# The order of the mixer's last three tiles in a pooling-mixer and gated-FFN trunk

## The chip, the cores and the metric

One core of a Trainium2 chip runs the whole program. The metric is device microseconds (us) of that core, as the median of several runs. TensorE is called PE in the profile, its weight loads PEld, VectorE DVE, ScalarE ACT, GpSimd POOL, and SyncE, which issues most DMAs, SP.

## The reference

The input is 1024 tokens of 1024 features in float32, and there is one layer of depth. It computes:

```
h  = rms_norm(x, norm_mix_g)
y  = pool_scale * (windowed mean of h (2, 4, 8, 16 tokens) - h) @ pool_w + pool_b     (4 groups of 256 features)
x1 = x + y
n  = rms_norm(x1, norm_ffn_g)
h2 = causal depthwise conv of width 3 over (n @ w_in)      w_in: 1024 x 5632
out = x1 + (silu(gate) * val) @ w_out                      val, gate: the halves of h2; w_out: 2816 x 1024
```

## The kernel before

**Stages.** Eight token tiles of 128 rows pass through the mixer. Then comes the first FFN product, 44 column blocks of 128 handled as 22 pairs n, and last the second product. Both are seven-product (Winograd) schemes: each 2 x 2 block product is made of seven products P1 to P7 of sums of blocks. Each of those takes its operands split in a head (rounded to float32r by ScalarE) and a remainder (source minus head, VectorE), and is 12 matmuls of 128 x 512.

**The mixer, tile j** (line numbers are those of the profile). `mixer_window` (L221) makes the window sums on TensorE (psd). `mixer_out` (L240) multiplies by the pool weights (psy, L247 and L250), adds the residual on VectorE (x, L253), stores it, and asks ScalarE for the row's square sum (junk, L154) and square root (L155), VectorE for the small steps after them (st, L156 to L159). `ffn_norm` (L257) writes the normalised tile (n2, L261). `ffn_operand` (L272) turns it with eight transposes into a PSUM pair of banks (pst, L276).

**What is made of a turned tile.** Tiles 0 to 3 give the FFN's blocks B11 and B21 with their splits. Tiles 4 to 7 give, together with tile j - 4, the block sums in n2f: `b22` is copied out by ScalarE (L287), then VectorE subtracts `b12` (in pst) from `b11` (L288), ScalarE and VectorE split that sum into T1 (L289: head L295, remainder L296), and VectorE makes two more differences (L290, L291). The first of those two is the last reader of the tile's PSUM banks.

**The FFN's weight side.** `prep_in` (L332) splits a weight block or a sum of weight blocks (S1 to S4) into a head and a remainder (`split`, L74, lines L76 and L77). For the first two pairs the sums themselves are made by accumulating DMAs; from the third pair on VectorE adds them (L310).

**The products around the change.** `events` (L418) is an order written by hand: P1 of pairs 0 and 1 (into banks X0, X1), P2 of both (X0, X1 again), P5 of both (T1 with S1, into Z0, Z1), P3 of both (B22 with S4), then P6, P7, P4 of pair 0 and of pair 1, and pairs 2 to 21 after them. The first three events stand in the mixer's loop, for its steps 8, 10 and 11. P5's banks Z lie in the PSUM space that the mixer's pool (ps_p, with pst) gives back, so their first matmul needs the last readers of pst to be done. A weight head takes a slot of a ring of seven (`hl`); x7 occupies one such slot until n2_7 has been made.

**What sets the order.** A scheduler orders the instructions of each engine; the code gives it the dependencies, and `tc.issue_after(mark)` queues what is recorded inside it behind the marked instruction on that instruction's engine (order only, no wait). Each engine then works through its own queue in that order, so an instruction that waits holds up all behind it.

Of the kernel before, what the change touches and what calls it, by code (L numbers as in the profile page):

```python
# [18 lines left out]
NS = S // P  # L19
NK = D // P  # L20
# [28 lines left out]
def trunk_kernel(ctx: ExitStack, tc: tile.TileContext, x, consts, par, rows, pool_w, w_in, w_out, out):  # L49
    nc = tc.nc  # L50
# [14 lines left out]
    def bank2(name):  # L65
        return ps_p.tile([P, 2 * NH], F32, tag="ps", name=name)
# [77 lines left out]
    ident = cst[:, :FAC]  # L144
# [4 lines left out]
    marks = {}  # L149
# [69 lines left out]
    ds, gains = {}, []  # L219
# [37 lines left out]
    def ffn_norm(j):  # L257
        x1, r = n2s[j]
        n2 = n2s[j] = pp.tile([P, D], F32, tag="n2", name=f"n2_{j}", bufs=2)
        nc.vector.tensor_tensor(r[1], r[0], r[1], ALU.mult)  # L260
        nc.vector.scalar_tensor_tensor(n2, x1, r[1], gains[0], op0=ALU.mult, op1=ALU.mult)  # L261
# [7 lines left out]
    for b in ("B11", "T1", "B21"):  # L269
        nops[b] = nop_tile(nop_a, b)  # L270

    def ffn_operand(j):  # L272
        n2 = n2s.pop(j)
        ps = bank2(f"pst{j}")
        for c in range(NK):
            nc.tensor.transpose(ps[:, c * P : (c + 1) * P], n2[:, c * P : (c + 1) * P], ident)  # L276
        cols = slice(j * P, (j + 1) * P)
        ps3 = ps.rearrange("p (c s) -> p c s", c=NK)
        lo, hi = slice(0, 4), slice(4, 8)
        if j < NS // 2:  # L280
# [6 lines left out]
        nc.scalar.activation(b22, ps3[:, hi, :], AF.Copy)  # L287
        sub(b11, b11, b12)  # L288
        split_n(nops["T1"], b11, cols0)  # L289
        sub(n2f[:, lo, cols], b22, b12)  # L290
        sub(b21, b22, b21)  # L291

    def split_n(t, src, cols=slice(None), ks=slice(None)):
        h = t[:, 0, ks, cols]
        nc.scalar.activation(h, src, AF.Copy)  # L295
        nc.vector.tensor_tensor(t[:, 1, ks, cols], src, h.bitcast(F32), ALU.subtract)  # L296


    order = [j + k * NP2 for j in range(NP2) for k in range(2)]
    raws, sums, aops = {}, {}, {}  # L300
# [3 lines left out]
        nc.sync.dma_start(raws[n], w_in[order[n]])  # L304

    def sub(out, a, b):
        nc.vector.tensor_tensor(out, a, b, ALU.subtract)  # L307

    def add(out, a, b):
        nc.vector.tensor_tensor(out, a, b, ALU.add)  # L310
# [1 line left out]
    def tmp(name):  # L312
        return work.tile([P, NH], F32, tag="sum", name=name, bufs=3)
# [18 lines left out]
    def prep_in(n, op):  # L332
        a11, a12, a21, a22 = (raws[n][:, i, k * NH : (k + 1) * NH] for i in range(2) for k in range(2))
        if op in ("S1", "S2") and (n, "S3") not in sums:
            s3 = sums[n, "S3"] = tmp(f"S3_{n}")
            add(s3, a11, a21)
            add(a21, a21, a22)
        if op in ("S2", "S4") and (n, "S2") not in sums:
            sums[n, "S2"] = a11
            add(a11, a21, a11)  # L340
        if op == "S4" and (n, "S4") not in sums:
            add(a12, a12, a11)
        if op == "S3":
            src = sums[n, "S3"]
        else:
            src = {"A11": a11, "A12": a12, "S1": a21, "A22": a22, "S2": a11, "S4": a12}[op]
        aops[n, op] = split(src, f"{op}s_{n}")
        if op == "A22" and n + 2 < NF:
            load_in(n + 2)

    def product(bank, a, b, opens):
        m = 0
        for k in range(4):
            ks = slice(k * P, (k + 1) * P)
            for i, l in ((0, 0), (0, 1), (1, 0)):
                nc.tensor.matmul(bank, a[:, i, ks], b[:, l, k, :], start=opens and m == 0, stop=m == 11, skip_group_check=not opens)  # L356
# [8 lines left out]
    def small(tag, name, bufs):  # L365
        return work.tile([P, NH], F32, tag=tag, name=name, bufs=bufs)

    def step(n, p):
        a, b, z = STEPS[p]
        opens = p in ("P1", "P6", "P5")  # L370
        if opens:
            pool = ps_x if z == "X" else ps_yz
            banks[n, z] = pool.tile([P, NH], F32, tag=z, name=f"{z}{n}")
        bank = banks[n, z]
        product(bank, aops.pop((n, a)), nops[b], opens)
        tt = nc.vector.tensor_tensor
        if p == "P1":
            hid[n, "q1"] = small("q1", f"q1_{n}", 2)
            nc.scalar.activation(hid[n, "q1"], bank, AF.Copy, scale=-1.0)
        elif p == "P2":  # L380
            hid[n, "a"] = work.tile([P, S], F32, tag="ha", name=f"ha{n}", bufs=1)
            nc.scalar.activation(hid[n, "a"][:, :NH], bank, AF.Copy)
        elif p == "P6":
            hid[n, "q2"] = tmp(f"q2_{n}") if n < 2 else late.tile([P, NH], F32, tag="q2", name=f"q2_{n}", bufs=2)
            tt(hid[n, "q2"], bank, hid[n, "q1"], ALU.subtract)
            if n < 2:
                tt(hid[n, "a"][:, NH:], banks[n, "Z"], hid[n, "q2"], ALU.add)
        elif p == "P5":
            hid[n, "r"] = left.tile([P, NH], F32, tag="r", name=f"r_{n}", bufs=2)
            tt(hid[n, "r"], hid[n, "q1"], bank, ALU.subtract)  # L390
        elif p == "P7":
            hid[n, "b"] = late.tile([P, S], F32, tag="hb", name=f"hb{n}", bufs=1)
            tt(hid[n, "b"][:, NH:], hid[n, "r"], bank, ALU.subtract)
# [67 lines left out]
    for j in range(2, NS + 4):  # L461
        if 2 < j < NS:
            mixer_norm(j)
        if 1 <= j - 1 < NS and j > 2:
            mixer_window(j - 1)
        if 1 <= j - 2 < NS:
            mixer_out(j - 2)
        if 0 <= j - 2 < NS:
            ffn_norm(j - 2)
        if 0 <= j - 4 < NS:  # L470
            ffn_operand(j - 4)
        if j in (4, 6):
            load_in(j // 2 - 2)
            sums_in(j // 2 - 2, 0)
        if 5 <= j <= 8:
            with tc.issue_after(marks[j - 2]), tc.issue_after(marks[f"b{j - 3}"]):
                prep_event(j - 5)
        if j in (7, 8):
            sums_in(j - 7, 1)
        if j in (8, 10, 11):  # L480
            event((8, 10, 11).index(j))
        with tc.issue_after(marks["edges"]):
            stat(j + 1)
            stat(j + 2)
# [15 lines left out]
    for ks in halves:  # L500
# [24 lines left out]
    def take(name):  # L525
# [113 lines left out]
    for k in range(-SLOOK, len(oevents)):  # L639
        p, f = oevents[k + SLOOK] if k + SLOOK < len(oevents) else (None, 0)  # L640
# [8 lines left out]
        with tc.issue_after(lasts[-1]) if lasts else nullcontext():  # L649
# [12 lines left out]
            p, f = oevents[k]  # L662
# [8 lines left out]
        set_, opens = chains[p]  # L671
# [17 lines left out]
        for i, g, c, bank in steps:  # L689
            a, b = oops[p, g]  # L690
            alone = opens and (p, i) != ("P4", 3)
            for m, (u, v) in enumerate(((0, 0), (0, 1), (1, 0))):
# [3 lines left out]
                    start=opens and first, stop=g == NP2 - 1 and m == 2, skip_group_check=not alone,  # L696
# [80 lines left out]
```

## Time and profile before

| | |
|---|---|
| Median of 3 runs | 705.21 us (705.0 to 705.26) |
| The profiled execution: its time, its span | 705.07 us, 702.9 us |
| PE, DVE, ACT busy in the span | 99%, 85%, 49% |
| PE's waits of the last mixer tiles and the first products | 1.2 us and 0.2 us, both at the start of P5 (Z) |
| Granted TensorE clock | 1.00 in all stretches asked |

In the rows of the timeline the first number is the start in us from the start of the span, the second the duration, then engine, line, operation, output and inputs by name without numbers (n is n2, a T or S stands for all tiles of that letter), partitions x elements and the count. In brackets is the idle time of the engine ahead of it and who ended it. Rows of VectorE operations of the same kind overlap a little: the next begins before the one ahead has ended.

### The profile page before, as it was taken

The numbers are of one execution on the slowest core, as the hardware profiler recorded it, in microseconds if no ns is written. First come the engines' busy times: TensorE is split into PE (matmuls) and PEld (weight loads), VectorE is DVE, ScalarE is ACT, GpSimd is POOL, SyncE is SP. The second block draws the span as 40 slices with busy tenths as digits, with TensorE's granted clock in tenths as the row PEclk, the third lists the DMA queues.
The fourth block names the chain that finished last, engine by engine and source line by source line (L and its number), as shares of the span: only waits on it lengthen the run. The fifth ranks groups of instructions, "written<-read, shape, count | busy, mean of one in ns | idle before, by whom it ended". The sixth has DMA issues, their size and how long they took to land.

```text
span 702.9 us, 8496 instructions
## 1 busy us (share of the span) xinstructions
PE 694.4 (99%) x3159; PEld 573.6 (82%) x3159; DVE 599.8 (85%) x884; ACT 343.1 (49%) x515; POOL 13.6 (2%) x32
## 2 busy tenths in 40 slices
PE   8999999999999999999999999999999999999997
PEld 5898788888888888888888888888888888888886
DVE  4688999999888888888888888876887988999985
ACT  5596546545444544444544444454554444444441
POOL 3110000000000000000000000000000000000000
PEclk9999999999999999999999999999999999999999
DMA  9953122132121122222222222229989700122121
GB/s 306 321 149 99 48 95 90 66 143 81 71 88 58 69 87 90 91 90 91 90 90 90 78 72 89 90 83 342 329 309 334 270 29 0 61 91 89 61 105 61
DMA packets 32586, 86.01 MB, mean 122 GB/s; under 512 B 3592, under 2 KB 5152, under 8 KB 29728
## 3 DMA queue, kind: packets, MB, share of 16 engines
q1 hardware_dynamic: 31296, 83.34, 33.2%
q0 software_dynamic: 1248, 2.11, 1.8%
q8 instruction: 25, 0.41, 0.2%
q14 instruction: 17, 0.14, 0.1%
HBM read 63.41 MB, written 19.92 MB: 119 GB/s over the span
## 4 chain that ended last, share of the span: by engine, by line
PE 95%; DMA 2%; DVE 1%; ACT 1%; issue 0%; SPq 0%; POOL 0%; DVEq 0%
PE oP L694 30%; PE Y L356 26%; PE Z L356 17%; PE X L356 16%; PE psy L247 3%; PE psd L176 2%; DMA x_edge<-in_x_dram 1%; PE pst L276 1%; DMA bias_hl<-rows_raw 1%; PE psy L250 1%; DVE n2f L307 0%; PE ps_edges L176 0%; DVE T L296 0%; PE ps_gain L214 0%; DVE n L261 0%
## 5 line engine op out<-in xcount | busy, mean ns | idle before, releaser
L694 PE MATMUL oP<-oBP,oAP 128*128 128x512 f32 (+1 forms) x924 | 208.9, 388 | 0.0
L694 PEld LDWEIGHTS oP<-oBP,oAP 128*128 128x128 f32 x924 | 172.9, 188 | 36.1 <-DVE oBP L77 0.3
L356 PE MATMUL Z<-T,S1s 128*128 128x512 f32 x264 | 64.1, 390 | 1.4 <-ACT T L295 1.2
L356 PE MATMUL X<-B,A11s 128*128 128x512 f32 x264 | 64.3, 390 | 0.0
L356 PE MATMUL Y<-T,S2s 128*128 128x512 f32 x264 | 64.0, 390 | 0.0
L356 PE MATMUL X<-B,A12s 128*128 128x512 f32 x264 | 63.5, 389 | 0.0
L356 PE MATMUL Y<-T,S3s 128*128 128x512 f32 x264 | 63.4, 389 | 0.0
L356 PE MATMUL Y<-T,A22s 128*128 128x512 f32 x264 | 63.4, 389 | 0.0
L356 PE MATMUL Z<-B,S4s 128*128 128x512 f32 x264 | 63.2, 389 | 0.0
L356 PEld LDWEIGHTS Z<-T,S1s 128*128 128x128 f32 x264 | 49.3, 188 | 12.6 <-ACT T L295 1.6
L356 PEld LDWEIGHTS Y<-T,S2s 128*128 128x128 f32 x264 | 49.4, 188 | 10.8 <-ACT S2s L76 0.4
L356 PEld LDWEIGHTS Y<-T,S3s 128*128 128x128 f32 x264 | 49.5, 188 | 10.3
L356 PEld LDWEIGHTS Y<-T,A22s 128*128 128x128 f32 x264 | 49.6, 188 | 10.3
L356 PEld LDWEIGHTS Z<-B,S4s 128*128 128x128 f32 x264 | 49.5, 188 | 10.3
L356 PEld LDWEIGHTS X<-B,A12s 128*128 128x128 f32 x264 | 49.5, 188 | 10.2
L356 PEld LDWEIGHTS X<-B,A11s 128*128 128x128 f32 x264 | 49.4, 188 | 10.2
L76 ACT ACTIVATE oBP<-blk 128x512 fp32r<-128x512 f32 x53 | 33.5, 633 | 49.1 <-PE oP L694 32.2
L77 DVE TENSOR_TENSOR oBP<-blk,oBP 128x512 fp32r<-128x512 f32 x53 | 36.7, 692 | 13.0 <-ACT oBP L76 13.0
L414 ACT ACTIVATE gate<-gate 128x1024 f32<-128x1024 f32 x22 | 23.3, 1061 | 44.8 <-DVE gate L405 44.5
L76 ACT ACTIVATE oAP<-blk 128x512 fp32r<-128x512 f32 x55 | 34.1, 621 | 18.9 <-DVE blk L307 15.9
L310 DVE TENSOR_TENSOR win<-win 128x512 f32<-128x512 f32 x60 | 41.3, 689 | 1.1
L77 DVE TENSOR_TENSOR oAP<-blk,oAP 128x512 fp32r<-128x512 f32 x55 | 37.8, 687 | 2.6 <-ACT oAP L76 2.6
(125 smaller groups left out, 942.5 us busy)
## 6 DMA issues: line engine op xcount, KB each, us to landing
win<-in_w_in_dram SPq DMA_DIRECT2D x22, 1024.0 KB, 4.8
g_dram<-val SPq DMA_DIRECT2D x22, 512.0 KB, 2.6
blk<-g_dram SPq DMA_DIRECT2D x33, 256.0 KB, 5.3
blk<-in_w_out_dram SPq DMA_DIRECT2D x31, 256.0 KB, 5.8
A12s<-g_dram SPq DMA_DIRECT2D x22, 256.0 KB, 5.2
B21s<-in_w_out_dram SPq DMA_DIRECT2D x22, 256.0 KB, 2.7
x<-in_x_dram SPq DMA_DIRECT2D x8, 512.0 KB, 9.5
x_dram<-x SPq DMA_DIRECT2D x8, 512.0 KB, 2.6
```

What stands on the lines that cost most here:

```text
L76: nc.scalar.activation(t[:, 0, :], src, AF.Copy)
L77: m = nc.vector.tensor_tensor(t[:, 1, :], src, t[:, 0, :].bitcast(F32), ALU.subtract)
L176: m = nc.tensor.matmul(ps[:, c * P : (c + 1) * P], src[:, c * P : (c + 1) * P], weights[:, c // 2, :], start=True, stop=True)
L247: nc.tensor.matmul(o, dh[:, c, :], wps[:, c, :], start=c % 4 == 0, stop=False, skip_group_check=True)
L250: m = nc.tensor.matmul(ps[:, cols], ones, bias_hl[:, cols], start=False, stop=True, skip_group_check=True)
L276: nc.tensor.transpose(ps[:, c * P : (c + 1) * P], n2[:, c * P : (c + 1) * P], ident)
L310: nc.vector.tensor_tensor(out, a, b, ALU.add)
L356: nc.tensor.matmul(bank, a[:, i, ks], b[:, l, k, :], start=opens and m == 0, stop=m == 11, skip_group_check=not opens)
L414: nc.scalar.activation(gate, gate, AF.Silu)
L694: nc.tensor.matmul(bank, a[:, u, i * P : (i + 1) * P], b[:, v, c], start=opens and first, stop=g == NP2 - 1 and m == 2, skip_group_check=n ...
```

## The change

Five edits, all in the order of the work; no operation on data is added or taken away.

- The tile's transposes (`ffn_turn`) and the work on a turned tile (`ffn_operand`) are separate now. For tiles 4 to 7 the latter has two parts: part 0 is b11 - b12 and the split of T1, part 1 is the copy of b22 and the other two differences. Part 0 comes first in all four tiles.
- The normalisation of tile 7 is queued right behind tile 5's differences, and takes its small steps at once.
- The splits of both S1 (first used by P5) are queued right behind n2_6, which puts them ahead of the last residual (x7).
- Tile 7's transposes are recorded inside P2 of pair 0 (`between`, after its sixth matmul), where they had stood in P2 of pair 1.
- Part 0 of tiles 6 and 7 follows n2_7, part 1 of both follows T1 of tile 7, and the prepared weights of the next events (from S4 on) follow T1 of tile 7 as well.

The core of the diff:

```diff
+    def ffn_operand(j, parts=(0, 1)):
...
-        nc.scalar.activation(b22, ps3[:, hi, :], AF.Copy)
-        sub(b11, b11, b12)
-        split_n(nops["T1"], b11, cols0)
-        sub(n2f[:, lo, cols], b22, b12)
-        sub(b21, b22, b21)
+        if 0 in parts:
+            sub(b11, b11, b12)
+            marks[f"T1_{j}"] = split_n(nops["T1"], b11, cols0)
+        if 1 in parts:
+            nc.scalar.activation(b22, ps3[:, hi, :], AF.Copy)
+            sub(n2f[:, lo, cols], b22, b12)
+            marks[f"rest_{j}"] = sub(b21, b22, b21)
...
+            if between and k == 1:
+                with tc.issue_after(last.ins):
+                    between()
...
-        if 0 <= j - 2 < NS:
-            ffn_norm(j - 2)
-        if 0 <= j - 4 < NS:
-            ffn_operand(j - 4)
+        if j == 9:
+            ffn_turn(5)
+            with tc.issue_after(marks[7]):
+                ffn_operand(5)
+            with tc.issue_after(marks["rest_5"]):
+                ffn_norm(7)
+        elif j == 10:
+            ffn_turn(6)
...
-        if j in (8, 10, 11):
-            event((8, 10, 11).index(j))
+        if j == 8:
+            with tc.issue_after(marks["n2_6"]):
+                prep_event(4)
+                prep_event(5)
+            event(0)
+        if j == 10:
+            event(1)
+        if j == 11:
+            event(2, between=lambda: ffn_turn(7))
+            with tc.issue_after(marks["n2_7"]):
+                ffn_operand(6, (0,))
+                with tc.issue_after(marks["T1_6"]):
+                    ffn_operand(7, (0,))
+            with tc.issue_after(marks["T1_7"]):
+                ffn_operand(6, (1,))
+                ffn_operand(7, (1,))
...
-    for k in range(4, 4 + LOOK):
-        with tc.issue_after(marks[NS - 1]):
+    for k in range(6, 4 + LOOK):
+        with tc.issue_after(marks["T1_7"]):
             prep_event(k)
```

**VectorE around the last residual.** Before, from n2_6 to T1 of tile 5 (x7 is the residual, n2f with pst5 the first two differences of tile 5, S1s the remainder of a split S1):

```order
L261 SCALAR_TENSOR_TENSOR n2_6_641<-x6_149,st_b6_635,gain_b_305 128x1024
L253 TENSOR_TENSOR x7_151<-psy7_679,x7_151 128x1024
L77 TENSOR_TENSOR S1s_0_791<-win0_419,S1s_0_791 128x512
L307 TENSOR_TENSOR n2f_163<-n2f_163,pst5_702 128x4x128 x2
L307 TENSOR_TENSOR n2f_163<-n2f_163 128x4x128
L156 TENSOR_SCALAR st_b7_693<-st_b7_693 128x1
L296 TENSOR_TENSOR T1_165<-n2f_163,T1_165 128x4x128
```

In the changed kernel, the same place:

```order
L261 SCALAR_TENSOR_TENSOR n2_6_641<-x6_149,st_b6_635,gain_b_305 128x1024
L77 TENSOR_TENSOR S1s_0_664<-win0_419,S1s_0_664 128x512
L77 TENSOR_TENSOR S1s_1_667<-win1_544,S1s_1_667 128x512
L253 TENSOR_TENSOR x7_151<-psy7_685,x7_151 128x1024
L315 TENSOR_TENSOR n2f_163<-n2f_163,pst5_705 128x4x128
L304 TENSOR_TENSOR T1_165<-n2f_163,T1_165 128x4x128
L156 TENSOR_SCALAR st_b7_699<-st_b7_699 128x1
L315 TENSOR_TENSOR n2f_163<-n2f_163,pst5_705 128x4x128
```

Two S1 remainders moved ahead of x7. Between x7 and the remainder of T1 there stood four operations of 512 elements, and now one.

**VectorE from n2_7 on.** Before:

```order
L261 SCALAR_TENSOR_TENSOR n2_7_699<-x7_151,st_b7_693,gain_b_305 128x1024
L296 TENSOR_TENSOR T1_165<-n2f_163,T1_165 128x4x128
L77 TENSOR_TENSOR S1s_1_794<-win1_544,S1s_1_794 128x512
L77 TENSOR_TENSOR S4s_0_797<-win0_419,S4s_0_797 128x512
L77 TENSOR_TENSOR S4s_1_800<-win1_544,S4s_1_800 128x512
L307 TENSOR_TENSOR n2f_163<-n2f_163,pst7_747 128x4x128 x2
L307 TENSOR_TENSOR n2f_163<-n2f_163 128x4x128
L77 TENSOR_TENSOR S2s_0_803<-win0_419,S2s_0_803 128x512
L296 TENSOR_TENSOR T1_165<-n2f_163,T1_165 128x4x128
```

In the changed kernel:

```order
L261 SCALAR_TENSOR_TENSOR n2_7_720<-x7_151,st_b7_699,gain_b_305 128x1024
L315 TENSOR_TENSOR n2f_163<-n2f_163,pst6_723 128x4x128
L304 TENSOR_TENSOR T1_165<-n2f_163,T1_165 128x4x128
L315 TENSOR_TENSOR n2f_163<-n2f_163,pst7_753 128x4x128
L77 TENSOR_TENSOR S3s_0_820<-S3_0_421,S3s_0_820 128x512
L304 TENSOR_TENSOR T1_165<-n2f_163,T1_165 128x4x128
L315 TENSOR_TENSOR n2f_163<-n2f_163,pst6_723 128x4x128
L315 TENSOR_TENSOR n2f_163<-n2f_163 128x4x128
L315 TENSOR_TENSOR n2f_163<-n2f_163,pst7_753 128x4x128
L315 TENSOR_TENSOR n2f_163<-n2f_163 128x4x128
L77 TENSOR_TENSOR S4s_0_797<-win0_419,S4s_0_797 128x512
```

Both T1 remainders come earlier, tile 6's directly behind the difference that it splits. The second read of pst7 was ahead of the last T1; it is now three operations behind it.

**ScalarE in the same stretch.** In the changed kernel, from tile 7's square on (before, the copy of pst5 stood ahead of the square, and the copy of pst6 behind it, ahead of tile 5's T1 head):

```order
L154 ACTIVATE junk_b7_698,st_b7_699<-x7_151 128x1024
L303 ACTIVATE T1_165<-n2f_163 128x4x128
L155 ACTIVATE st_b7_699<-st_b7_699,eps_t_154 128x1
L297 ACTIVATE n2f_163<-pst5_705 128x4x128
L390 ACTIVATE q1_1_745<-X1_732 128x512
L76 ACTIVATE S4s_1_800<-win1_544 128x512
L76 ACTIVATE S2s_0_803<-win0_419 128x512
L303 ACTIVATE T1_165<-n2f_163 128x4x128
L297 ACTIVATE n2f_163<-pst6_723 128x4x128
L393 ACTIVATE ha0_768<-X0_670 128x512
L76 ACTIVATE S3s_0_820<-S3_0_421 128x512
```

The head of T1 of tile 5 comes next behind the square of x7 now, and the head of S3 of pair 0 three places behind T1 of tile 6.

On TensorE the eight transposes of tile 7 come after the tenth of the twelve matmuls of P2 of pair 0 (before: after the third of pair 1), and P5's 24 matmuls run as two unbroken products (before: the first matmul of each, then the rest). From the third pair on all queues are as before.

More of the change, by code (lines that the diff above doesn't have):

```diff
@@ L260, in ffn_norm @@
         nc.vector.tensor_tensor(r[1], r[0], r[1], ALU.mult)
-        nc.vector.scalar_tensor_tensor(n2, x1, r[1], gains[0], op0=ALU.mult, op1=ALU.mult)
+        marks[f"n2_{j}"] = nc.vector.scalar_tensor_tensor(n2, x1, r[1], gains[0], op0=ALU.mult, op1=ALU.mult).ins
     n2f = n2_pool.tile([P, NK, S], F32, tag="n2f", name="n2f")
@@ L270, in trunk_kernel, with ffn_turn @@
         nops[b] = nop_tile(nop_a, b)
-    def ffn_operand(j):
+    turned = {}
+    def ffn_turn(j):
         n2 = n2s.pop(j)
@@ L275, in ffn_operand @@
         for c in range(NK):
-            nc.tensor.transpose(ps[:, c * P : (c + 1) * P], n2[:, c * P : (c + 1) * P], ident)
-        cols = slice(j * P, (j + 1) * P)
-        ps3 = ps.rearrange("p (c s) -> p c s", c=NK)
+            m = nc.tensor.transpose(ps[:, c * P : (c + 1) * P], n2[:, c * P : (c + 1) * P], ident)
+        marks[f"pst{j}"] = m.ins
+        turned[j] = ps.rearrange("p (c s) -> p c s", c=NK)
+    def ffn_operand(j, parts=(0, 1)):
+        ps3, cols = turned[j], slice(j * P, (j + 1) * P)
         lo, hi = slice(0, 4), slice(4, 8)
@@ L295, in split_n @@
         nc.scalar.activation(h, src, AF.Copy)
-        nc.vector.tensor_tensor(t[:, 1, ks, cols], src, h.bitcast(F32), ALU.subtract)
+        return nc.vector.tensor_tensor(t[:, 1, ks, cols], src, h.bitcast(F32), ALU.subtract).ins
     order = [j + k * NP2 for j in range(NP2) for k in range(2)]
@@ L306, in sub @@
     def sub(out, a, b):
-        nc.vector.tensor_tensor(out, a, b, ALU.subtract)
+        return nc.vector.tensor_tensor(out, a, b, ALU.subtract).ins
     def add(out, a, b):
@@ L349, in prep_in, with product @@
             load_in(n + 2)
-    def product(bank, a, b, opens):
+    def product(bank, a, b, opens, between):
         m = 0
@@ L355, in product @@
             for i, l in ((0, 0), (0, 1), (1, 0)):
-                nc.tensor.matmul(bank, a[:, i, ks], b[:, l, k, :], start=opens and m == 0, stop=m == 11, skip_group_check=not opens)
+                last = nc.tensor.matmul(bank, a[:, i, ks], b[:, l, k, :], start=opens and m == 0, stop=m == 11, skip_group_check=not opens)
                 m += 1
+            if between and k == 1:
+                with tc.issue_after(last.ins):
+                    between()
     STEPS = {
@@ L366, in small, with step @@
         return work.tile([P, NH], F32, tag=tag, name=name, bufs=bufs)
-    def step(n, p):
+    def step(n, p, between=None):
         a, b, z = STEPS[p]
@@ L374, in step @@
         bank = banks[n, z]
-        product(bank, aops.pop((n, a)), nops[b], opens)
+        product(bank, aops.pop((n, a)), nops[b], opens, between)
         tt = nc.vector.tensor_tensor
@@ L426, in prep_event, with event @@
             prep_in(n, STEPS[p][0])
-    def event(k):
+    def event(k, between=None):
         if k >= 4:
@@ L431, in event @@
         n, p = events[k]
-        step(n, p)
+        step(n, p, between)
         if p == "P4":
@@ L467, in trunk_kernel @@
             mixer_out(j - 2)
-        if 0 <= j - 2 < NS:
-            ffn_norm(j - 2)
-        if 0 <= j - 4 < NS:
-            ffn_operand(j - 4)
+        if j == 9:
[6 more added lines that the diff above has]
+            ffn_turn(6)
+        else:
+            if 0 <= j - 2 < NS:
+                ffn_norm(j - 2)
+            if 0 <= j - 4 < NS - 1:
+                ffn_turn(j - 4)
+                ffn_operand(j - 4)
         if j in (4, 6):
```

## The prediction

> **What bounds the kernel now.** I read the page first, then TensorE's waits, then busy time by stretch, then the timelines of three engines around the change.
>
> ```profile
> span 702.9 us, 8496 instructions
> PE 694.4 (99%) x3159; PEld 573.6 (82%) x3159; DVE 599.8 (85%) x884; ACT 343.1 (49%) x515; POOL 13.6 (2%) x32
> ```
>
> TensorE is the bound. What is left to win near the change is its idle time there, in the list of TensorE's waits:
>
> ```profile
> PE Z L356 <- ACT T L295: 1.2, 1, 1.2
> PE Z L356 <- DVE T L296: 0.2, 1, 0.2
> ```
>
> Both lie at the start of P5, which needs T1. But busy time by stretch (PE, PEld, DVE, ACT, POOL; clock; DMA share; GB/s) shows a second full engine:
>
> ```profile
> 70.00:80.00 10.00, 8.87 (x43) 6.86 (x41) 9.96 (x20) 7.96 (x16) 0.00 (x0) 1.00 0.13 50
> 90.00:100.00 10.00, 10.00 (x45) 8.26 (x44) 9.85 (x12) 4.12 (x5) 0.00 (x0) 1.00 0.30 105
> 100.00:110.00 10.00, 10.00 (x44) 7.69 (x43) 10.00 (x14) 5.54 (x8) 0.00 (x0) 1.00 0.00 1
> 130.00:700.00 570.00, 569.11 (x2519) 471.15 (x2517) 490.07 (x685) 262.06 (x384) 0.00 (x0) 1.00 0.33 116
> ```
>
> From 70 to 110 us VectorE is as full as TensorE. From 130 us on TensorE hardly pauses, so whatever is lost or won by then stays. TensorE's timeline over this stretch:
>
> ```profile
> 76.55 2.32 PE L356 MATMUL X<-B,A12s 128*128 128x512 f32 x9
> 80.09 0.73 PE L356 MATMUL Z<-T,S1s 128*128 128x512 f32 x2 [1.22 <-ACT T L295]
> 81.05 5.28 PE L356 MATMUL Z<-T,S1s 128*128 128x512 f32 x22 [0.22 <-DVE T L296]
> 86.17 5.60 PE L356 MATMUL Z<-B,S4s 128*128 128x512 f32 x24
> 91.61 0.62 PE L356 MATMUL Y<-T,S2s 128*128 128x512 f32 x2
> 102.51 2.88 PE L356 MATMUL Y<-T,A22s 128*128 128x512 f32 x12
> 105.34 0.73 PE L356 MATMUL Y<-T,S2s 128*128 128x512 f32 x2
> ```
>
> Unhindered, 24 matmuls take 5.44 us (86.17 to 91.61), 0.227 each. Twelve from 102.51 would hand over at 105.23; the next starts at 105.34, and it waits for this chain, in the timelines of VectorE and ScalarE:
>
> ```profile
> 101.48 0.68 DVE L393 TENSOR_TENSOR hb<-r,Y 128x512 f32<-128x512 f32 x1
> 103.87 0.69 DVE L310 TENSOR_TENSOR win<-win 128x512 f32<-128x512 f32 x1
> 104.65 0.63 ACT L76 ACTIVATE S2s<-win 128x512 fp32r<-128x512 f32 x1 [2.41 <-DVE win L310]
> ```
>
> VectorE's sum of weight blocks ends at 104.56, ScalarE's head at 105.28, the matmul starts at 105.34. So at 105 us VectorE's queue already sets TensorE's time, and the question is not how early T1 comes but **how early or late VectorE's whole queue gets to that sum**. The same instructions stand ahead of it in both kernels; only waits inside VectorE's queue can move it.
>
> **VectorE, part by part.** Its timeline, the parts that the change touches:
>
> ```profile
> 60.34 1.23 DVE L253 TENSOR_TENSOR x<-psy,x 128x1024 f32<-128x1024 f32 x1 [0.76 <-PE psy L250]
> 61.49 0.68 DVE L77 TENSOR_TENSOR A12s<-win,A12s 128x512 fp32r<-128x512 f32 x1
> 65.19 1.28 DVE L261 SCALAR_TENSOR_TENSOR n<-x,st_b,gain_b 128x1024 f32<-128x1024 f32 x1
> 67.91 1.23 DVE L253 TENSOR_TENSOR x<-psy,x 128x1024 f32<-128x1024 f32 x1 [1.44 <-PE psy L250]
> 69.05 0.68 DVE L77 TENSOR_TENSOR S1s<-win,S1s 128x512 fp32r<-128x512 f32 x1
> 69.65 1.28 DVE L307 TENSOR_TENSOR n2f<-n2f,pst 128x512 f32<-128x512 f32 x2
> 71.64 0.69 DVE L296 TENSOR_TENSOR T<-n2f,T 128x512 fp32r<-128x512 f32 x1
> 76.10 0.69 DVE L77 TENSOR_TENSOR S1s<-win,S1s 128x512 fp32r<-128x512 f32 x1
> 76.70 1.29 DVE L77 TENSOR_TENSOR S4s<-win,S4s 128x512 fp32r<-128x512 f32 x2
> 77.91 1.28 DVE L307 TENSOR_TENSOR n2f<-n2f,pst 128x512 f32<-128x512 f32 x2
> ```
>
> Prices: an operation of 512 elements takes 0.60 from start to start (76.10 to 76.70), a residual 1.14 to 1.15 and 1.23 to its end. ScalarE's side, around tile 7's square:
>
> ```profile
> 69.28 1.05 ACT L154 ACTIVATE junk_b<-x 128x1024 bf16<-128x1024 f32 x1
> 70.22 0.19 ACT L154 ACTIVATION_READ_ACCUMULATOR junk_b<-x 128x1 f32 x1
> 70.32 0.59 ACT L287 ACTIVATE n2f<-pst 128x512 f32<-128x512 f32 x1
> 70.98 0.62 ACT L295 ACTIVATE T<-n2f 128x512 fp32r<-128x512 f32 x1
> ```
>
> The square holds ScalarE for 1.04 (69.28 to 70.32), a T1 head takes 0.62 and ends at 71.60, and VectorE's remainder follows 0.04 later (71.64).
>
> *S1 remainders ahead of x7: gain 1.44.* VectorE idles for 1.44 ahead of 67.91. Two remainders are 1.20 and, with the wait of the next item, fill it: n2_6 ends its slot at 66.5, plus 0.7, plus 1.2 is 68.4, after psy7 is there. So x7 starts 0.3 to 0.5 late and the hole is gone.
>
> *T1 of tile 4: loss 0.7.* From x6 the remainder needs 1.23 (residual), about 0.1 of handing over, 1.04 (square, ahead of the head on ScalarE), 0.62 and 0.04: 3.0 after x6's start. VectorE has only one difference and A12s between them, free at 1.15 + 2 x 0.60 = 2.35. It waits 0.65 to 0.7. Before, the tile's two other differences stood there too and covered this.
>
> *T1 of tile 5: loss 1.25.* The same 3.0 after x7, but one operation between: free at 1.75. Before, S1s and three differences (69.05 to 71.45) covered it. Queued behind the waiting remainder are tile 7's small steps and n2_7, and so T1 of tiles 6 and 7.
>
> *T1 of tile 6: loss 0.78.* Its remainder stands directly behind its difference: 0.69 + 0.04 + 0.62 + 0.03 = 1.38 from start to start in place of 0.60.
>
> *S3 of pair 0: loss 0.3.* On ScalarE its head follows T1's head, a copy and ha; three slots of about 0.5 put its end 1.5 behind T1's head, where VectorE comes after 1.2.
>
> *T1 of tile 7:* its head follows S3's at once; no wait. The work put behind it is only reordered. Transposes of tile 7 inside another product: same count and same two changes between transposes and products, nothing. TensorE will wait about 0.6 there for n2_7, in a stretch where it later waits for VectorE anyway; without that cover it would cost those 0.6.
>
> Sum on VectorE: 0.7 + 1.25 + 0.78 + 0.3 - 1.44 = **1.6 late**. Of that a pause of VectorE later on may take something back:
>
> ```profile
> 92.03 2.36 DVE L296 TENSOR_TENSOR T<-n2f,T 128x1024 fp32r<-128x1024 f32 x2
> 94.53 0.69 DVE L385 TENSOR_TENSOR q<-Y,q 128x512 f32<-128x512 f32 x1
> ```
>
> Ahead of q it stands still from about 94.3 (92.03 + 2.36, less the overlap) to 94.53, some 0.1 to 0.2. I take 1.5.
>
> [...] In this trace the next one starts 0.09 before the end (76.10 + 0.69 against 76.70), so the measured 0.60 is used; at 0.69 a slot tile 6's loss would be 0.69 and the sum 1.5.
>
> **TensorE, place by place.** *P5 opens.* Its bank needs tile 7's second PSUM read, which now stands behind T1: x7 at 68.3; T1 of tile 5 3.0 later, 71.3; three slots and the small steps later (2.4) n2_7, 73.7; its 1.2 and tile 6's difference with its wait (1.38) later T1 of tile 6, 76.3; a difference and S3 with its wait (0.6 + 0.9) and the slot ahead of them later T1 of tile 7, 78.4; and 3 x 0.60 later the read, 80.2 to 80.9. P5 starts at 80.9 where it had started at 80.09. Once started it runs through: the second pause (81.05) is gone, since T1 is long done. 24 matmuls and a restart of 0.1 end at 86.45 in place of 86.17: **0.3 late**, though T1 itself came 1.5 earlier. *P4* (102.51) needs hb (101.48, ends 102.16): with VectorE 1.5 late it starts at 103.7. *P6 of pair 2* (105.34) needs the sum of weights: 105.34 + 1.5 = 106.8. After it both engines run as before, 1.5 later, and TensorE never catches up.
>
> So 705.07 + 1.5 = 706.6 for an execution like the profiled one; the median of the runs shown is 0.14 above that one, hence **706.7**.
>
> **Rivals.**
>
> 1. *VectorE recovers part.* If ScalarE's handing over is quicker than in the rows above, or pauses absorb more, VectorE is late by 0 to 0.8 and only P5's 0.3 and the pause at 105 remain: 705.3 to 706.0. For it: ScalarE is 49% busy. Against it: in the three stretches from 70 to 110 us shown VectorE idles for 0.04, 0.15 and 0 us, which leaves nothing to absorb with. It decides if the four losses come to under 2.3.
>
> 2. *Not slower: the T1 waits don't happen.* If VectorE finds each head ready, the 1.44 hole is filled and nothing is paid: the whole queue is 1.44 early, the sum of weights too, and P5's holes (1.22 and 0.22) close under it. Time 705.07 - 1.44 = 703.6, or 703.8 with the median's offset; it comes out under the old time as soon as the four losses stay below 1.44. Against it: a head cannot start before the square of the same residual on ScalarE, and before the change that took until 71.60, 3.7 after x7. [...]
>
> 3. *Worse.* S2's head of pair 0 needs the slot that x7 frees when n2_7 ends, and stands ahead of T1 of tile 6 on ScalarE. If that holds T1 of tiles 6 and 7 up by 0.5 each, VectorE is 2.5 late: 707.7.
>
> **Chances.** The forecast, 0.8 to 2.3 late (706.0 to 707.5): 0.66. Rival 1: 0.17. Rival 2: 0.10. Rival 3: 0.07. A measurement of this kernel can tell about 0.2%, 1.4 us, from no change, and the forecast sits just above that line: about two thirds of its chance (0.45) and all of rival 3 lie above, 0.52 slower. Rival 2 passes the line on the other side only at its full price, 0.05 faster. The rest, 0.43, is within 0.2%. The range leaves out rival 2 and the far end of rival 3: 705.3 to 707.7.
>
> **What would show it.** Right: in the changed profile VectorE waits for ScalarE's T1 at T1 of tiles 4, 5 and 6, for 0.7, 1.2 and 0.8; x7 has no idle time ahead; TensorE's wait at Z names a difference of n2f and not T, and Z runs its 24 matmuls in one piece from about 80.9; Y with S2 of pair 2 starts near 106.8. Wrong: TensorE at 105.34 or earlier there, or VectorE's waits for T1 under 0.4 each.

## The result, and the profile after

| | before | after |
|---|---|---|
| Median, 13 runs each | 705.20 us (704.75 to 705.49) | 706.83 us (706.0 to 707.17) |
| Ratio after to before | | 1.0023, 95% interval 1.0016 to 1.0030 |
| Profiled execution: time, span | 705.07 us, 702.9 us | 707.07 us, 705.0 us |

The change makes the kernel 1.6 us slower, against the 1.5 of the forecast, and the interval of the ratio lies above 1. The granted clock of each of the 13 runs of after is 0.999 or 1.000, so none of the loss is a lower clock. The profiled execution of after starts with a difference that is not the change's: x6, the residual ahead of everything that was moved, begins at 60.83 where it began at 60.34. In the executions of the experiments below, whose kernels are alike up to there, it begins between 59.89 and 60.56. So from here on times of different executions are compared **from the start of x6**; for after and before that means taking 0.49 off.

TensorE's waits, all of them from 60 to 110 us:

```profile
PE Z L364 <- DVE n2f L315: 1.7, 1, 1.7
PE Y L364 <- ACT val L414: 0.8, 1, 0.8
PE pst L278 <- DVE n L261: 0.3, 1, 0.3
```

The wait at Z names a difference of n2f where it named T twice before; T1 is no longer what P5 waits for. In all, TensorE waits longer than before: 2.8 us against 1.4. Its timeline shows where:

```profile
75.37 1.06 PE L278 MATMUL pst<-cst,n 128*128 128x128 f32 x8 [0.26 <-DVE n L261]
81.32 5.69 PE L364 MATMUL Z<-T,S1s 128*128 128x512 f32 x24 [1.66 <-DVE n2f L315]
86.84 5.60 PE L364 MATMUL Z<-B,S4s 128*128 128x512 f32 x24
104.40 3.00 PE L364 MATMUL Y<-T,A22s 128*128 128x512 f32 x12 [0.79 <-ACT val L414]
107.42 0.74 PE L364 MATMUL Y<-T,S2s 128*128 128x512 f32 x2
```

P5 runs in one piece now (x24 in one row). From x6 it opens 0.74 later than before (20.49 against 19.75) and ends 0.18 later, since its second pause is gone. The product at 107.42 is the handover that the prediction rests on: 46.59 from x6 against 45.00, **1.59 late**. So most of the loss arises between P5's end and this place. ScalarE's head and VectorE's sum ahead of it:

```profile
105.96 0.68 DVE L318 TENSOR_TENSOR win<-win 128x512 f32<-128x512 f32 x1
```

```profile
106.74 0.63 ACT L76 ACTIVATE S2s<-win 128x512 fp32r<-128x512 f32 x1 [2.41 <-DVE win L318]
```

The chain is that of before: sum, head, matmul within 1.5 us, and VectorE's sum comes 1.60 later from x6 (45.13 against 43.53). Why it is late can be read in VectorE's timeline:

```profile
60.83 1.22 DVE L253 TENSOR_TENSOR x<-psy,x 128x1024 f32<-128x1024 f32 x1 [0.77 <-PE psy L250]
62.57 0.69 DVE L77 TENSOR_TENSOR A12s<-win,A12s 128x512 fp32r<-128x512 f32 x1
63.79 0.69 DVE L304 TENSOR_TENSOR T<-n2f,T 128x512 fp32r<-128x512 f32 x1 [0.54 <-ACT T L303]
67.39 1.29 DVE L77 TENSOR_TENSOR S1s<-win,S1s 128x512 fp32r<-128x512 f32 x2
68.59 1.22 DVE L253 TENSOR_TENSOR x<-psy,x 128x1024 f32<-128x1024 f32 x1
69.73 0.68 DVE L315 TENSOR_TENSOR n2f<-n2f,pst 128x512 f32<-128x512 f32 x1
71.55 0.69 DVE L304 TENSOR_TENSOR T<-n2f,T 128x512 fp32r<-128x512 f32 x1 [1.14 <-ACT T L303]
75.14 0.68 DVE L315 TENSOR_TENSOR n2f<-n2f,pst 128x512 f32<-128x512 f32 x1
76.52 0.69 DVE L304 TENSOR_TENSOR T<-n2f,T 128x512 fp32r<-128x512 f32 x1 [0.70 <-ACT T L303]
77.12 0.68 DVE L315 TENSOR_TENSOR n2f<-n2f,pst 128x512 f32<-128x512 f32 x1
78.08 0.69 DVE L77 TENSOR_TENSOR S3s<-S,S3s 128x512 fp32r<-128x512 f32 x1 [0.28 <-ACT S3s L76]
80.50 0.68 DVE L315 TENSOR_TENSOR n2f<-n2f,pst 128x512 f32<-128x512 f32 x1
```

x7 (68.59) has no idle time ahead any more: the S1 remainders fill it. In its place stand four waits in brackets, three for the heads of T1 of tiles 4, 5 and 6 and one for the head of S3. The head of tile 5's T1 stands on ScalarE behind the square of x7, which had to wait for x7:

```profile
69.84 1.06 ACT L154 ACTIVATE junk_b<-x 128x1024 bf16<-128x1024 f32 x1 [4.26 <-DVE x L253]
70.90 0.61 ACT L303 ACTIVATE T<-n2f 128x512 fp32r<-128x512 f32 x1
```

Busy time by stretch says the same in two rows:

```profile
70.00:80.00 10.00, 9.39 (x45) 7.25 (x44) 7.81 (x16) 7.96 (x15) 0.00 (x0) 1.00 0.13 52
130.00:700.00 570.00, 570.00 (x2520) 471.94 (x2519) 491.24 (x686) 264.29 (x386) 0.00 (x0) 1.00 0.32 115
```

From 70 to 80 us VectorE falls from 9.96 to 7.81 of 10, in the stretch in which it had no time to give away; from 130 to 700 us TensorE never pauses, so nothing is caught up.

### The profile page after: what moved, and what is told of

It reads as the page before. It is cut to its first block, busy times and chain, and to the rows that moved or that the text cites. A ratio compares the mean times of both kernels' runs of the same rounds, so it can differ in the third digit from the quotient of the medians.

```text
span 705.0 us, 8501 instructions
## 1 busy us (share of the span) xinstructions
PE 693.9 (98%) x3158; PEld 573.4 (81%) x3159; DVE 600.1 (85%) x884; ACT 343.1 (49%) x515; POOL 13.4 (2%) x32
## 4 chain that ended last, share of the span: by engine, by line
PE 92%; DVE 3%; DMA 2%; ACT 2%; issue 1%; SPq 0%; POOL 0%; DVEq 0%
PE oP L729 30%; PE Y L364 24%; PE Z L364 17%; PE X L364 15%; PE psy L247 3%; PE psd L176 2%; DVE T L304 1%; DMA x_edge<-in_x_dram 1%; DMA bias_hl<-rows_raw 1%; DVE n2f L315 1%; PE psy L250 0%; PE pst L278 0%; ACT T L303 0%; DVE x L253 0%; ACT junk_b L154 0%
```

## The experiments

**Theory Q** is that of the prediction: VectorE's whole queue is late by its waits, and its sum of weight blocks for the third pair sets TensorE near 107 us (the handover). **Theory P** is the obvious other reading of the list of waits: the longest wait, at Z, is the loss, because the second PSUM read of tile 7 (80.50) holds the bank space of P5 and now comes late. **Rival C** is that a wait costs nothing and only the number of operations counts.

Nine kernels ran, each five rounds beside the kernel before on the same chip. The second and third columns are from x6 in the profiled execution, as differences from before (P5's first matmul 19.75, handover 45.00); the last is the difference of the medians.

| kernel | P5 opens | handover of pair 2 | time | median, ratio to before (95%) |
|---|---|---|---|---|
| after | +0.74 | +1.59 | +1.63 | 706.83, 1.0023 (1.0016 to 1.0030) |
| e1_tile7_first | +0.74 | +1.62 | +1.82 | 706.88, 1.0025 (1.0016 to 1.0034) |
| e2_r_twice | +0.73 | +2.34 | +2.46 | 707.52, 1.0031 (1.0020 to 1.0043) |
| e5_reads_first | +0.14 | +1.40 | +1.33 | 706.57, 1.0021 (1.0012 to 1.0030) |
| e6_fill_waits | +0.75 | +0.22 | 0.00 | 705.24, 1.0000 (0.9992 to 1.0009) |
| e7_whole_tiles | -1.37 | -0.60 | -0.63 | 704.61, 0.9996 (0.9988 to 1.0005) |
| e8_turn_in_pair1 | +1.88 | +4.42 | +5.53 | 710.77, 1.0070 (1.0053 to 1.0086) |
| e9_parts_first | +0.26 | -0.23 | -0.28 | 704.76, 0.9996 (0.9987 to 1.0005) |
| e3_s1_ahead | -0.01 | other order there | +1.26 | 706.32, 1.0010 (1.0002 to 1.0019) |
| e4_t1_7_prompt | -1.22 | -1.03 | -1.05 | 704.01, 0.9985 (0.9976 to 0.9993) |

Read down the columns: the time goes with the handover to some 0.2 us in every row that has both but e8's, whose runs spread over 4 us, and does not go with P5's opening. VectorE's sum goes with the handover to 0.01 us in all these rows (its start from x6, less before's 43.53: +1.60 in after, +2.35 in e2, +1.41 in e5, +0.23 in e6, -1.02 in e4).

Which engine held the other up is a second question. P5 ends where P3 (Z with S4) starts, at 86.17 in before. From there to the handover TensorE takes 19.17 us in before, e4 and e6 and 19.16 in e9, but 20.58 to 21.03 in after, e1, e2, e5, e7 and e8. In the first four kernels the list of waits has none for TensorE in between, and VectorE pauses 0.22 to 0.25 ahead of q (at 94.53 in before), which needs TensorE's next product. In e6 the row names it:

```profile
94.73 0.69 DVE L400 TENSOR_TENSOR q<-Y,q 128x512 f32<-128x512 f32 x1 [0.17 <-PE Y L368]
```

So there are two bounds. Where VectorE's queue is in time, P5's end sets the handover; where it is later, VectorE does. In after, P5's end is 0.18 late and VectorE brings the other 1.41.

**e1: tile 7's rest ahead of tile 6's.** The changed kernel with the rest of tile 7 ahead of that of tile 6:

```diff
             with tc.issue_after(marks["T1_7"]):
+                ffn_operand(7, (1,))
                 ffn_operand(6, (1,))
-                ffn_operand(7, (1,))
```

> The changed kernel, with part 1 of tile 7 (the second read of its PSUM banks) queued ahead of part 1 of tile 6; VectorE's operations and their sum are the same. Theory Q (VectorE's queue is late, and its sum of weight blocks for the third pair sets TensorE near 107 us): the read comes two slots, 1.2 us, earlier, the P5 product opens up to 1.2 earlier, and the time stays at the changed kernel's 706.8 within 0.2. Theory P (the second read holds P5's bank, and P5's late opening is the loss): about 1.2 faster, 705.6.

Measured 706.88: Q's number, yet the run decides nothing. P5 opened no earlier, still waiting 1.68 us for a difference of n2f. The bank space waits for the last reader of either tile, and tile 6's had only changed places with tile 7's.

**e2: r twice.** The changed kernel with r of the first two pairs (the difference that VectorE makes from P5's bank, L401) computed twice, so two more VectorE operations of 512 elements behind P5's opening:

```diff
-            tt(hid[n, "r"], hid[n, "q1"], bank, ALU.subtract)
+            for _ in range(2 if n < 2 else 1):
+                tt(hid[n, "r"], hid[n, "q1"], bank, ALU.subtract)
```

> The changed kernel, with the difference r (line 401) of pairs 0 and 1 computed twice: two more VectorE operations of 512 elements, 0.60 us each, behind the second PSUM read of tile 7 and ahead of the third pair's sums. Theory Q: TensorE is later by the 1.2 us of the two operations, 708.0 (707.8 to 708.2). Theory P: P5 opens as before and TensorE has the products of P3 to cover them: 706.8, no change.

Measured 707.52, 0.7 above after: P's "no change" is out, Q's direction is right and its size was too large. (The intervals of the two ratios overlap, but beside e1, which has after's time and ran on the same chip, the runs hardly do: 706.72 to 707.32 there, 707.26 to 707.57 here.) P5 opens where it did in after, and the handover comes 0.75 later. The missing 0.45 is found in after's VectorE queue, where it pauses shortly three times behind P5's opening. A slot, the time from the start of one operation to the start of the next, is 0.60, or 1.14 for the remainder of 1024 elements at 94.25; what the starts lie further apart is the pause:

```profile
86.37 0.68 DVE L77 TENSOR_TENSOR A22s<-win,A22s 128x512 fp32r<-128x512 f32 x1
87.04 0.69 DVE L401 TENSOR_TENSOR r<-q,Z 128x512 f32<-128x512 f32 x1
...
90.52 0.69 DVE L77 TENSOR_TENSOR S3s<-S,S3s 128x512 fp32r<-128x512 f32 x1
91.38 2.36 DVE L304 TENSOR_TENSOR T<-n2f,T 128x1024 fp32r<-128x1024 f32 x2 [0.17 <-ACT T L303]
...
94.25 1.22 DVE L304 TENSOR_TENSOR T<-n2f,T 128x1024 fp32r<-128x1024 f32 x1
95.49 0.69 DVE L396 TENSOR_TENSOR q<-Y,q 128x512 f32<-128x512 f32 x1
```

0.07, 0.26 and 0.10: together 0.43, and 1.20 less 0.43 is 0.77, beside the 0.75 measured. My expectation had left these pauses out.

**e5: both PSUM reads first.** The mended e1: in the changed kernel the second PSUM reads of tiles 6 and 7 stand ahead of the two differences that read no PSUM (part 2 is the difference without PSUM, which stood in part 1):

```diff
-            sub(n2f[:, lo, cols], b22, b12)
+            marks[f"read_{j}"] = sub(n2f[:, lo, cols], b22, b12)
+        if 2 in parts:
             marks[f"rest_{j}"] = sub(b21, b22, b21)
...
             with tc.issue_after(marks["T1_7"]):
                 ffn_operand(6, (1,))
+            with tc.issue_after(marks["read_6"]):
                 ffn_operand(7, (1,))
+            with tc.issue_after(marks["read_7"]):
+                ffn_operand(6, (2,))
+                ffn_operand(7, (2,))
```

> The changed kernel with the second PSUM reads of tiles 6 and 7 both queued ahead of the two differences that read no PSUM: tile 7's read, the last one on P5's bank space, comes one slot of 0.60 us earlier, whichever of the two tiles the space waits for. Theory Q (VectorE's whole queue is late, and the sum of weight blocks of the third pair sets TensorE near 107 us): the same operations stand ahead of that sum, so 706.8. Theory P (the late opening of P5 is the loss): P5 opens at 80.7 in place of 81.3, and the time falls by 0.6 to 706.2.

P5 opens 0.60 earlier than in after, as meant:

```profile
80.33 5.70 PE L365 MATMUL Z<-T,S1s 128*128 128x512 f32 x24 [1.06 <-DVE n2f L316]
...
106.84 0.73 PE L365 MATMUL Y<-T,S2s 128*128 128x512 f32 x2
```

The handover gains 0.19 of it, and the time is 706.57, 0.3 below after by the medians and by the ratios within each other's interval. Opening P5 0.60 earlier brings less than half of what P asks for.

**e6: the waits filled.** The changed kernel with S4's remainder of pair 0 in tile 5's wait and that of pair 1 in tile 6's; the same operations, in another order:

```diff
-            sub(b11, b11, b12)
-            marks[f"T1_{j}"] = split_n(nops["T1"], b11, cols0)
+            with tc.issue_after(sub(b11, b11, b12)):
+                if j in (5, 6):
+                    prep_event(j + 1)
+            with tc.issue_after(splits[-1]) if j in (5, 6) else nullcontext():
+                marks[f"T1_{j}"] = split_n(nops["T1"], b11, cols0)
...
-        aops[n, op] = split(src, f"{op}s_{n}")
+        aops[n, op] = split(src, f"{op}s_{n}", splits)
...
-    for k in range(6, 4 + LOOK):
+    for k in range(8, 4 + LOOK):
```

> The changed kernel with the remainder of S4 of pair 0 queued between tile 5's first difference and its T1 remainder, and that of pair 1 likewise in tile 6, where VectorE waits 1.14 and 0.70 us for ScalarE's heads. No operation more or fewer. Theory Q: two slots of 0.60 fill 1.2 of those 1.84, VectorE reaches the sum of weight blocks 1.2 earlier, and the time falls to 705.6; if later pauses give back part of it, as they took 0.4 of 1.2 when r was computed twice, to 706.0. Rival C (a wait costs nothing, operations are to be counted): 706.8. Theory P does not differ from Q here, since tile 7's read comes earlier as well.

VectorE's timeline at the two places:

```profile
69.22 0.68 DVE L319 TENSOR_TENSOR n2f<-n2f,pst 128x512 f32<-128x512 f32 x1
69.81 0.68 DVE L77 TENSOR_TENSOR S4s<-win,S4s 128x512 fp32r<-128x512 f32 x1
71.04 0.69 DVE L308 TENSOR_TENSOR T<-n2f,T 128x512 fp32r<-128x512 f32 x1 [0.54 <-ACT T L307]
...
74.63 0.68 DVE L319 TENSOR_TENSOR n2f<-n2f,pst 128x512 f32<-128x512 f32 x1
75.23 0.69 DVE L77 TENSOR_TENSOR S4s<-win,S4s 128x512 fp32r<-128x512 f32 x1
76.01 0.69 DVE L308 TENSOR_TENSOR T<-n2f,T 128x512 fp32r<-128x512 f32 x1
```

From difference to remainder it takes 1.82 and 1.38 as in after (69.73 to 71.55, 75.14 to 76.52), so the two slots of 0.60 are free. TensorE:

```profile
80.82 5.72 PE L368 MATMUL Z<-T,S1s 128*128 128x512 f32 x24 [1.68 <-DVE n2f L319]
...
105.54 0.73 PE L368 MATMUL Y<-T,S2s 128*128 128x512 f32 x2
```

This is the run that decides. I had expected it not to tell Q from P, which was wrong: the S4 remainders that moved forward had stood *behind* the read of tile 7, so the read comes no earlier and **P5 opens within 0.01 us of its place in after and with the same wait (1.68, there 1.66)**. Yet the handover comes 1.37 earlier and the time falls by 1.6, to that of before: the two slots give 1.20, and of the later pauses that e2 found 0.17 come back. P, which rests on P5's opening and so sees no change here, falls; C falls too, since no operation was removed. The wait at Z is the longest in TensorE's list, and with P5 open 0.75 later than before, P5's end and this kernel's handover are both 0.22 late: that is what the late opening costs here.

**e7: whole tiles.** The changed kernel with each tile's work in the order of before (copy, first difference, T1, the other two differences). Of the fifth edit, which queues the two parts of tiles 6 and 7 apart, only the place of the whole tiles is left (tile 6 behind n2_7, tile 7 behind T1 of tile 6); the other edits are kept:

```diff
-        if 0 in parts:
-            sub(b11, b11, b12)
-            marks[f"T1_{j}"] = split_n(nops["T1"], b11, cols0)
-        if 1 in parts:
-            nc.scalar.activation(b22, ps3[:, hi, :], AF.Copy)
-            sub(n2f[:, lo, cols], b22, b12)
-            marks[f"rest_{j}"] = sub(b21, b22, b21)
+        nc.scalar.activation(b22, ps3[:, hi, :], AF.Copy)
+        sub(b11, b11, b12)
+        marks[f"T1_{j}"] = split_n(nops["T1"], b11, cols0)
+        sub(n2f[:, lo, cols], b22, b12)
+        marks[f"rest_{j}"] = sub(b21, b22, b21)
...
-                ffn_operand(6, (0,))
-                with tc.issue_after(marks["T1_6"]):
-                    ffn_operand(7, (0,))
-            with tc.issue_after(marks["T1_7"]):
-                ffn_operand(6, (1,))
-                ffn_operand(7, (1,))
+                ffn_operand(6)
+            with tc.issue_after(marks["T1_6"]):
+                ffn_operand(7)
```

> The changed kernel without the edit that puts T1's part first: each tile's copy, three differences and T1 in the order of before, all else as changed (S1 remainders ahead of x7, n2_7 behind tile 5's differences, tile 7's transposes in pair 0). Theory Q: the waits at T1 of tiles 4, 5 and 6 (0.54, 1.14 and 0.70 us) lose their reason and the 1.44 ahead of x7 stays filled; the sum of weight blocks comes 2.0 to 2.4 earlier than in the changed kernel, but TensorE can win there only the 0.11 to 0.5 us by which it waits for VectorE beyond its own work: 704.4 to 704.8. Theory P: P5 opens when tile 7 has been read, now ahead of T1 of tile 7: near 79, 2 us earlier, 704.8. If the parts-first edit costs nothing and the loss comes from the other four edits: 706.8.

Measured 704.61, 2.2 below after: the waits for the heads of T1 are gone, x7 has 0.22 ahead of it in place of 1.44, and P5 opens without any wait. The loss lies with putting T1 first and queueing the rest behind it. P5's end is 2.01 earlier than before and the handover only 0.60, so here too VectorE sets it. The ratio's interval against before still holds 1, so that this version beats before is not shown.

**e8: the transposes back in pair 1.** The changed kernel with tile 7's transposes in P2 of pair 1:

```diff
-            event(2, between=lambda: ffn_turn(7))
+            event(2)
+            event(3, between=lambda: ffn_turn(7))
...
-    event(3)
```

> The changed kernel with tile 7's transposes back inside P2 of pair 1 (the other four edits kept). The prediction put the move of the transposes at nothing, with the note that a cover might go. Theory Q: n2_7 stands ahead of these transposes in both, but T1 of tiles 6 and 7 and P5's bank space wait for them: the transposes come about 2.3 us later (ten matmuls of 0.227), VectorE's second half of tile 7 stands still for what is not filled, and the time rises by 1.0 to 2.3 to 707.8 to 709.1. If the move is free: 706.8.

Measured 710.77 (707.57 to 711.75). The direction is Q's, the size is larger, and the profiled execution (709.32) shows why: P5 opens 1.14 later than in after, behind 3.27 us in which TensorE stands still, and its first 24 matmuls then take 7.19 us in place of 5.52. Busy time by stretch has the granted clock in its eighth column:

```profile
82.00:84.00 2.00, 2.00 (x7) 1.56 (x7) 2.00 (x4) 0.09 (x1) 0.00 (x0) 0.63 0.00 0
84.00:86.00 2.00, 2.00 (x7) 1.56 (x6) 1.26 (x2) 0.00 (x0) 0.00 (x0) 0.52 0.00 0
```

1.14 and 1.67 are 2.81; the handover is 2.83 later than in after. The six runs spread with their mean granted clock: 707.57 at 0.999, 709.32 and 709.95 at 0.998, 711.60 to 711.75 at 0.995. So the run that lost hardly any clock is 0.7 above after's median, and what lies above that goes with the clock.

**e9: T1 first alone.** The kernel before with only the lines of `ffn_operand` in the new order, no queueing behind marks:

```diff
-        nc.scalar.activation(b22, ps3[:, hi, :], AF.Copy)
         sub(b11, b11, b12)
         split_n(nops["T1"], b11, cols0)
+        nc.scalar.activation(b22, ps3[:, hi, :], AF.Copy)
         sub(n2f[:, lo, cols], b22, b12)
         sub(b21, b22, b21)
```

> The kernel before with one edit alone: in each of tiles 4 to 7 the first difference and T1 are written ahead of the copy of b22 and the other two differences, with no queueing of the two parts behind marks. Theory Q: the order is not dear in itself, only where nothing is left to put into the wait. Here VectorE still has other work between: at tile 4 only A12s, as in the changed kernel (0.54 us of wait, which the 1.44 of idle time ahead of x7 takes back), at tile 5 three slots of 0.60, at tile 7 S4's and S2's remainders. So the queue is not late and the time stays at 705.0 to 705.5. If T1 first is itself the loss, as undoing that edit in the changed kernel won 2.2: 707.3. Theory P: the second read of tile 7 stands behind T1 here too, so P5 opens about 0.8 later than before, at 80.9: 705.9.

Measured 704.76, just under Q's band and no slower than before, though P5 opens 0.26 later: T1 first is not itself the loss, and P misses again. VectorE waits 0.54 at tile 4, as in after, and x7 still comes with psy7, so the idle time ahead of it shrinks by about as much:

```profile
63.29 0.69 DVE L296 TENSOR_TENSOR T<-n2f,T 128x512 fp32r<-128x512 f32 x1 [0.54 <-ACT T L295]
...
67.89 1.23 DVE L253 TENSOR_TENSOR x<-psy,x 128x1024 f32<-128x1024 f32 x1 [0.93 <-PE psy L250]
```

At tiles 5, 6 and 7 it waits nowhere for T1, since S1's, S4's and S2's remainders and differences of other tiles stand in between. So T1 first is dear only together with the edits that take this filling away, S1 ahead of x7 and everything else behind T1 of tile 7. Which of these two counts for more is not shown: neither was run alone with T1 first.

**e3 and e4: S1 ahead of x7, on the kernel before.** e3 has that edit alone. In e4 T1 of tile 7 is moved up as well, ahead of S3's remainder and of B22's:

```diff
+        if j == 8:
+            with tc.issue_after(marks["n2_6"]):
+                prep_event(4)
+                prep_event(5)
...
-    for k in range(4, 4 + LOOK):
+    for k in range(6, 4 + LOOK):
```

```diff
-    event(3)
-    event(4)
-    for ks in halves:
-        split_n(nops["B22"], b22[:, ks], ks=ks)
+    with tc.issue_after(marks["T1_7"]):
+        event(3)
+        event(4)
+        with tc.issue_after(marks["h7"]):
+            for ks in halves:
+                split_n(nops["B22"], b22[:, ks], ks=ks)
```

> The kernel before with one of the five edits alone: both S1 splits ahead of x7. VectorE's 1.44 of idle ahead of x7 shrinks to about 0.2 and its queue is 1.1 to 1.2 early from there on. Theory Q alone gives 705.2 - 1.1 = 704.1. But in its order T1 of tile 7 stands behind S2, S3 and the first B22 remainder, no earlier than before (near 80.9 against 80.3), so that P5's second pause grows by 0.6. If P5's opening is a second bound beside the queue, TensorE comes to 105 us late by that and no longer waits there: 705.2 to 705.5, and VectorE's gain is not seen.

> The kernel before with both S1 splits ahead of x7, and with T1 of tile 7 queued ahead of S3 of pair 0 and of B22's remainders. VectorE's queue is 1.2 early, with no wait for a T1 head, and T1 of tile 7 comes 1.2 earlier as well, near 79.1. Theory Q with P5's opening as second bound: both bounds move by 1.2, 704.0 (703.8 to 704.3), faster than both kernels. If neither the queue nor P5's opening set the time: 705.2.

e4 measured 704.01, as expected, the only version faster than before beyond its interval, and 2.8 below after. The hole (the idle time) ahead of x7 shrinks to 0.22, no T1 waits for a head, and of TensorE's 1.22 and 0.22 at P5 one wait of 0.41 is left. P5's end and the handover both come 1.03 earlier, as the bound of P5's end has it.

e3 missed: 706.32, with 5 of 11 runs at 704.70 to 705.63 and 6 at 706.32 to 707.06. The profiled execution is of the second kind. TensorE's timeline and its granted clock (the last column but two):

```profile
79.63 0.73 PE L356 MATMUL Z<-T,S1s 128*128 128x512 f32 x2 [1.20 <-ACT T L295]
81.12 6.90 PE L356 MATMUL Z<-T,S1s 128*128 128x512 f32 x22 [0.76 <-DVE T L296]
87.86 5.60 PE L356 MATMUL Z<-B,S4s 128*128 128x512 f32 x24
```

```profile
80.00:82.00 2.00, 1.24 (x5) 0.85 0.00 0
82.00:84.00 2.00, 2.00 (x6) 0.50 0.27 37
84.00:86.00 2.00, 2.00 (x8) 0.80 0.79 287
```

22 matmuls take 6.74 where 22 x 0.227 is 5.0: 1.7 lost to the clock, about what separates the two groups. The mean granted clock that is on record for each run separates the two groups: 0.999 to 1.000 in the five, 0.996 or 0.997 in the six. Without that loss this edit alone gains some 0.2 (704.88, the median of the five, against 705.06).

## Why the prediction was right, point by point

*What bounds the kernel* was right for a queue that comes late, which is what the change makes. e2 and e6 move the time by VectorE's queue with P5's opening fixed, and e5 moves P5's opening with little effect. That VectorE's queue "already" sets TensorE's time in before was half of it: VectorE itself pauses 0.23 there for a product behind P5, so an early queue wins little unless P5's end comes earlier too.

*The waits* came as priced. From start to start, less a slot, they are 0.62 at tile 4 (62.57 to 63.79), 1.22 at tile 5 (69.73 to 71.55), 0.78 at tile 6 (75.14 to 76.52) and 0.36 at S3 (77.12 to 78.08), together 2.98, against 0.7, 1.25, 0.78 and 0.3, together 3.03. The brackets show 0.54, 1.14, 0.70 and 0.28, since they count from an operation's end, which overlaps the next one by 0.09. The prediction's other value for a slot, 0.69, is shown by no run: four differences start at 79.30, 79.89, 80.50 and 81.09 here, 0.59 to 0.61 apart.

*The hole ahead of x7* is gone, but it was put at the bracket's 1.44 while the waits were priced from start to start. In that measure it was 1.52 (65.19 plus two slots to 67.91). The waits less the hole are thus 1.46, not 1.6.

*What a pause takes back* was put at 0.1 and went the other way. Counted as above, the pauses of VectorE behind P5's opening were 0.10 (ahead of r at 83.88) and 0.23 (ahead of q at 94.53) before, 0.33 together; after, they are the three of e2, 0.43. So they cost 0.10 more.

*Tile 7's small steps* were costed at nothing, and over both tiles that is right. The last two have nothing between them any more ahead of n2_7:

```profile
73.55 0.15 DVE L159 RECIPROCAL st_b<-st_b 128x1 f32<-128x1 f32 x1
73.74 0.16 DVE L260 TENSOR_TENSOR st_b<-st_b 128x1 f32<-128x1 f32 x1
73.94 1.28 DVE L261 SCALAR_TENSOR_TENSOR n<-x,st_b,gain_b 128x1024 f32<-128x1024 f32 x1
```

They cost 0.39 here and 0.15 before, where differences stood between them. Other steps of tiles 6 and 7 became cheaper by as much: the eight steps together cost 1.18 before and 1.18 after.

*The sum* is then 1.46 + 0.10 = 1.56, beside 1.60 measured on VectorE. That the forecast's 1.5 came so near is in part luck: its waits less the hole were 0.1 too large, its pauses 0.2 too small.

*TensorE's places*, on before's scale (0.49 off): P5 opens at 80.83 (forecast 80.9), in one piece, 0.18 late at its end (0.3); P4 starts at 103.91 (103.7), P6 of pair 2 at 106.93 (106.8). The profile puts P4's wait down to ScalarE's val, where the prediction named hb; val ends at 104.33 and hb at 104.25 (103.57 + 0.68), and both come late by VectorE's queue.

*The transposes* were put at nothing. Their place adds no work, and TensorE waits 0.26 for n2_7 (forecast 0.6) under the wait at Z. But e8 shows that with the other edits made it is needed: without it P5 opens 1.1 later, and TensorE lost clock in five of the six runs. A move was costed alone that pays only beside the others.

*The rivals.* Rival 1 (pauses give back up to 1.5) did not happen. Rival 2's price, the hole filled with nothing paid, is real only in part: with the hole filled and no wait for a T1 head, e4 and e7 give -1.05 and -0.63 of its 1.44. e4 needed T1 of tile 7 moved up for it, and e3, the hole filled alone, gives some -0.2 at full clock. Against rival C stands e6: the same operations, 1.2 us of waits filled, 1.6 us faster. In the changed kernel VectorE's waits for another engine's results are paid in full (2.98 us, less the hole's 1.52, beside a sum that comes 1.60 late), and operations alone don't tell the time. Rival 3's coupling is there but small: S2's head starts at 75.25, right behind n2_7's end, and T1 of tile 6 follows it at 75.85; VectorE waited there no longer than forecast.

## What to carry to other kernels

The longest wait in the bound engine's list need not be the loss (1.68 us at Z in e6, which runs in before's time): look for the next place where another full engine hands over to it, and count that engine's queue from a common mark to there. Before a step is brought forward on such an engine, count the operations that are left between it and what it waits for; each slot missing (0.60 us here) is paid, unless an idle time further on takes it back, as the one ahead of x7 did in e9 (1.44 to 0.93 us, for a wait of 0.54). Then look whether the bound engine would itself be there later: a queue that is made earlier than that wins little (e3 filled 1.20 us of idle time and won some 0.2). Price holes and waits in one measure, from start to start.

## What the runs showed of the hardware

TensorE's granted clock fell to 0.50 behind pauses: in e3 behind 1.20 and 0.76 us with two matmuls between, in e8 behind 3.27. In stretches of half a microsecond it stays below 1.00 from about 81.4 to 84.8 us in e3 and from 82.5 to 85.9 in e8, about 3.4 us both times, and matmuls start 0.43 us apart in place of 0.227 (from 81.6 to 84.3 in e3, from 83 to 85.4 in e8). In e8 it falls only 0.7 us after the pause has ended. Single pauses of 1.58 to 1.68 us (e1, e2, e6, e9, after) and before's 1.22 and 0.22 left it at 1.00 in the stretches behind them. It is not the same in every run of a kernel: beside e3 and e8, one run of e5's ten (708.78, at 0.997) and two of e7's eleven (706.58 and 706.75, at 0.996 and 0.998) show a lower mean clock than the 0.999 to 1.000 of the others. Where it fell in these three is not known, as none of them was profiled. What makes it fall is not shown: in e3's profile two pauses of together 1.96 us came ahead of the fall, while a single one of 1.68 was followed by none in e1 and e6, and five of e3's eleven runs kept 0.999 or 1.000.
